# A four-wide second projection group in the first mixer unit, and later HGRN2 threads

## The chip, the cores and the metric

The kernel is one launch on one core of a Trainium2 chip. The metric is device time in microseconds (us) of one execution. The engines are named as in the profile: PE multiplies matrices into PSUM banks and loads its weights through PEld; DVE and ACT do elementwise work and are the only ones here that empty PSUM banks; POOL clears a few tiles; SP issues all DMAs. Each engine takes its instructions strictly in the order in which the program holds them, and an instruction that must wait for another engine holds up everything behind it on its own engine.

## What is computed

One layer of a decoder trunk, for 272 prompt tokens (16 of them meta tokens) and 8 single sample tokens that share all weights: a SwiGLU half-step, a mixer, a second SwiGLU half-step, each followed by a layer norm. Cut to what matters here:

```python
x = layer_norm(ALPHA * x + 0.5 * swiglu(x, f1_g, f1_u, f1_d), ln1_g, ln1_b)
q_r, k_r, v_r, g_r, q_h, f_h, i_h, g_h, a_r, a_h = jnp.split(x @ w_in, 10, axis=-1)   # 2048 wide each
f = lb + (1 - lb) * sigmoid(f_h);  k_h = 1 - f;  q_h = silu(q_h)
o_r, s_ret = retention(rotary(q_r), rotary(k_r) / 16, v_r, s_ret)                     # 8 heads of 256
o_h, s_hg = hgrn2(q_h, k_h, i_h, log(f), s_hg)                                        # 16 heads of 128
y = sigmoid(a_r) * head_ln(o_r) * silu(g_r) + sigmoid(a_h) * head_rms(o_h) * silu(g_h)
x = layer_norm(ALPHA * x + y @ w_out, ln2_g, ln2_b)
x = layer_norm(ALPHA * x + 0.5 * swiglu(x, f2_g, f2_u, f2_d), ln3_g, ln3_b)
```

The outputs are the new tokens and, for prompt and samples, the final states of both recurrences.

## The kernel before

**Dense work.** Activations stand with features on the 128 partitions and the 280 tokens along the row, in 16 pieces `xh[c]`, `xl[c]`: the high part in fp32r and the rest. Weights come as blocks of 128 x 128, eight to a DMA of 512 KB (`raw`). ACT casts each such unit to `whi` (L145), DVE subtracts to get `wlo` (L147), three buffers of each. `dense` (L162 to L174) multiplies: for each of 16 pieces k, and each block of a group, three matmuls into one PSUM bank, `whi` x `xh`, `whi` x `xl`, `wlo` x `xh` (L169, L170, L171). A group of n blocks is thus 16 steps of 3n matmuls. A matmul streams 280 columns, or 264 where the 16 meta tokens are not needed (the names in `LIVE`).

**PSUM.** Eight banks stand in two pools of four: `acc_bank` for dense outputs, `mx_bank` for the mixer's small matmuls and, of unit 0, for the `i_h` group. A pool hands its banks round; a matmul that starts in a bank waits until the last reader of what it held is through.

**The mixer.** It runs over eight units u, each one retention head and two HGRN2 heads. `project` computes the six projections f, q_h, i_h, q_r, k_r, v_r in groups of two blocks (`qkv_groups`), and, one unit later, the four gates (`gate_groups`). `evacuate` empties the banks. After `i_h` it starts a generator `mix_hg`, after `v_r` one called `mix_ret`: threads that hold the recurrences' small work. `dense` calls `pump` after each step k; `pump` counts each thread down by one and runs it to its next `yield` when its count is out. A `yield 14` therefore means "go on 14 dense steps later". This sets the order on PE, which is the order in which the code runs. DVE, ACT and SP get their order from a scheduler that reads the same code; it is fixed in the built program.

`mix_hg` transposes v (`pt`), after a yield multiplies products against ones (`pd`, and `pl` of its first level), goes through seven levels of a scan (`pl`), and then for each of two heads: transposes K (`ptk`), loads and updates the sample states (`smh`), yields, makes the prompt state (`pst`, copied to `Sh`), yields 10, multiplies queries by the sample states (`pq`), yields 3, makes the output (`po`), yields 7, sums squares (`pv`) and normalises. The gates' `evacuate` needs the threads' outputs: `while u not in done: pump()` (L513) runs a thread on at once, with no dense step between, where it has not finished.

**The start of the mixer.** The first four blocks of unit 0, f and q_h, are multiplied while the first layer norm is unfinished, on data before the mean is taken off; `Norm.first` (L294 to L314) then calls `normalise`, which makes the final `xh[c]` and `xl[c]` for 16 pieces (on DVE L191, L320, L324 for each, on ACT L323), and only then corrects the four outputs: DVE reads each bank in L309 (`pj_f`, `pj_q_h`). These four outputs fill all four banks of `acc_bank`.

Of the kernel before, what the change touches and what calls it, by code (L numbers as in the profile page):

```python
# [20 lines left out]
KC = D // P  # L21
DFF = 5504
FC = DFF // P
NMETA, SEQ, NS = 16, 256, 8
LP = NMETA + SEQ
T = LP + NS
# [39 lines left out]
QKV_ORDER = ["f", "q_h", "i_h", "q_r", "k_r", "v_r"]  # L66
LIVE = {"q_r", "q_h", "g_r", "g_h", "a_r", "a_h"}
# [3 lines left out]
def qkv_groups(u):  # L71
    gs = [[(n, 2 * u), (n, 2 * u + 1)] for n in QKV_ORDER]
    if u == 0:
        gs = [gs[0] + gs[1]] + gs[2:]
    return gs


# [20 lines left out]
def trunk(ctx: ExitStack, tc: tile.TileContext, A, O):  # L98
# [62 lines left out]

    def dense(block, nk, outs, xhi, xlo, cols=slice(0, T), hook=None):  # L162
        n = len(outs)
        for k in range(nk):
            for i in range(n):
                wh, wl = block()
                h, l = xhi[k][:, cols], xlo[k][:, cols]
                o = outs[i][:, : h.shape[1]]
                nc.tensor.matmul(o, wh, h, start=k == 0, stop=False)  # L169
                nc.tensor.matmul(o, wh, l, start=False, stop=False)  # L170
                nc.tensor.matmul(o, wl, h, start=False, stop=k == nk - 1)  # L171
            if hook is not None:
                hook(k)
# [32 lines left out]
    xh = [None] * KC  # L206
    xl = [None] * KC
# [176 lines left out]
    norm1 = ffn(1, A["w_up1"], A["w_dn1"], 1)  # L384


    with tc.tile_pool(name="yp", bufs=1) as yp:
        yh, yl = [None] * KC, [None] * KC
        with tc.tile_pool(name="mp", bufs=1) as mp:
# [27 lines left out]
            block = stream(A["w_in"])  # L417
            st = {}
# [31 lines left out]
            def start(gen, wait):  # L450
                threads.append([gen, wait])

            def project(groups):
                for grp in groups:
                    n = grp[0][0]
                    if len(grp) == 4:
                        outs = norm1.first(block, [acc_bank(f"pj_{n}{c}") for n, c in grp])
                    else:
                        bank = mx_bank if grp[0] == ("i_h", 0) else acc_bank
                        outs = [bank(f"pj_{n}{c}") for n, c in grp]  # L460
                        dense(block, KC, outs, xh, xl, slice(NMETA, T) if n in LIVE else slice(0, T), pump)
                    for j in range(0, len(grp), 2):
                        n = grp[j][0]
                        w0 = NMETA if n in LIVE and len(grp) == 4 else 0
                        w1 = w0 + (TL if n in LIVE else T)
                        evacuate(n, grp[j][1], grp[j + 1][1], outs[j][:, w0:w1], outs[j + 1][:, w0:w1])

            def evacuate(n, c0, c1, o0, o1):
                if n == "f":
                    f = tmp("f", (P, 2, T))  # L470
                    k = tmp("k", (P, 2, T))
# [7 lines left out]
                elif n == "q_h":  # L479
                    q = tmp("q", (P, 2, TL))  # L480
# [4 lines left out]
                elif n == "i_h":  # L485
                    v = tmp("v", (P, 2, T))
                    nc.scalar.copy(v[:, 0, :], o0)
                    nc.scalar.copy(v[:, 1, :], o1)
                    start(mix_hg(c0 // 2, st["f"], st["k"], st["q"], v), 3)
                elif n in ("q_r", "k_r"):  # L490
                    sc, w, x0 = (1.0, TL, NMETA) if n == "q_r" else (KSC, T, 0)
                    r = tmp(n, (P, 2, w))
# [6 lines left out]
                elif n == "v_r":  # L499
                    v = tmp("v", (P, 2, T))  # L500
# [3 lines left out]
                elif n in ("g_r", "g_h"):  # L504
# [7 lines left out]
                    u, e = divmod(c0, 2)  # L512
# [24 lines left out]
            def mix_hg(u, f, k, q, v):  # L537
# [23 lines left out]
                for h in range(2):  # L561
# [5 lines left out]
                    nc.scalar.copy(vm[:NMETA, h], pt[:NMETA, 2 * P :].rearrange("p (b f) -> p b f", b=2))  # L567
                    vrow.append(rows_out(vm[8:16, h, 1, :], P, f"vh{h}"))
                    yield 1
                yield 9 if u else 5  # L570
                pd = mx_bank("pd")
                sums(pd.rearrange("p (i c) -> p i c", i=2), hilo, slice(0, 2))
                nc.vector.tensor_tensor(
# [3 lines left out]
                for s in LEVELS:  # L577
# [5 lines left out]
                    for h in range(2 if s > 2 else 0):  # L583
                        for b in range(2):
                            k0, q0, o = NMETA + b * P, b * P, (2 * h + b) * min(s, 64)
                            if s == 64:
                                nc.tensor.matmul(
                                    pl[0:s, o : o + s], K[:, h, k0 : k0 + s], Q[:, h, q0 + s : q0 + 2 * s],
                                    start=True, stop=True)
# [5 lines left out]
                            else:  # L595
# [4 lines left out]
                                    start=True, stop=True)  # L600
# [4 lines left out]
                    n = LP - k0  # L605
                    nb = n // s
                    m = nb // 2
# [32 lines left out]
                for h in range(2):  # L640
# [14 lines left out]
                            out=sm[:, b, :], in0=vb[:, b, :], scalar=fk[:, 1, h, b : b + 1], in1=sm[:, b, :],  # L655
                            op0=ALU.mult, op1=ALU.add)
                    nc.sync.dma_start(O["sgs"][2 * u + h], sm)
                    yield 14 if u else 6

                    S = tmp("Sh", (P, 3, P))  # L660
                    pst = mx_bank("pst")
# [11 lines left out]
                    for b in range(NS):  # L673
# [3 lines left out]
                            start=b < 4, stop=b >= 4, tile_position=(0, j))  # L677
# [277 lines left out]
```

## Time and profile before

| | |
|---|---|
| median of 3 runs | 2826.17 us (2825.42 to 2827.91) |
| the profiled execution | 2827.42 us, its span in the profile 2825.5 us |
| PE busy | 2789.3 us, 99% of the span, 22642 matmul records |
| DVE, ACT busy | 1725.2 us (61%), 1354.2 us (48%) |
| mean granted PE clock | 0.996 |
| the mixer | about 812 to 1958 us of the span |

The profiled execution's time is 1.9 us more than its span, and 1.25 us more than the median of the runs. A busy time is the union of an engine's records. A matmul's record is longer (0.29 us) than the distance to the next one's start (0.129 us for 280 columns), because matmuls overlap; so time lost on PE is read from the starts. The waits list gives for each kind of instruction the idle time ahead of it and what ended it. The stage view gives busy times, counts and the granted clock of any stretch.

### The profile page before, as it was taken

Reading aid. Unit: us, or ns where it says so; the run is one execution under the profiler, and the core shown is the slowest. Engines: PE = TensorE matmul, PEld = TensorE weight load, DVE = VectorE, ACT = ScalarE, POOL = GpSimd, SP = SyncE. Lnnn points to the kernel's source line nnn. Section 1 sums busy time; section 2 is a strip of 40 time slices with the busy share of each in tenths; the row PEclk is TensorE's granted clock in tenths of the full one; section 3 lists DMA queues with packets and bytes.
Section 4 is the critical chain, followed back from the end, with each engine's and each line's share of the span. In section 5 each row is a group of like instructions: output and inputs, shape, how many; then the busy total and the mean of one; then the engine's idle time right before and its main releaser. Section 6 shows DMA issues by size and latency. Waiting matters only on the chain.

```text
span 2825.5 us, 54397 instructions
## 1 busy us (share of the span) xinstructions
PE 2789.3 (99%) x22642; PEld 2758.0 (98%) x22642; DVE 1725.2 (61%) x2786; ACT 1354.2 (48%) x2035; POOL 4.3 (0%) x42
## 2 busy tenths in 40 slices
PE   8999999999999999999999999999999999999997
PEld 8999999999999999999999999999999999999997
DVE  5444444455578777777777777775984444445555
ACT  4433344333355565656565656564554444443333
POOL 0000000000000000000000000000000000000000
PEclk9999999999999999999999999999999999999998
DMA  6555555555555675757575757575555555555543
GB/s 213 169 171 171 171 172 171 170 167 171 172 172 179 224 249 178 249 178 249 177 250 175 252 175 252 175 249 172 178 180 181 181 183 182 180 184 179 181 181 128
DMA packets 155718, 536.26 MB, mean 190 GB/s; under 512 B 18064, under 2 KB 27856, under 8 KB 155472
## 3 DMA queue, kind: packets, MB, share of 16 engines
q1 hardware_dynamic: 155472, 532.80, 55.5%
q8 instruction: 177, 2.90, 0.4%
q14 instruction: 69, 0.57, 0.1%
HBM read 502.12 MB, written 30.61 MB: 189 GB/s over the span
## 4 chain that ended last, share of the span: by engine, by line
PE 97%; DVE 1%; DMA 1%; ACT 0%; issue 0%; SPq 0%; ACTq 0%; DVEq 0%
PE up L170 12%; PE up L171 12%; PE up L169 12%; PE dn L169 6%; PE dn L170 6%; PE dn L171 6%; PE pj_g_r L169 1%; PE pj_v_r L169 1%; PE pj_f L169 1%; PE pj_g_h L169 1%; PE pj_k_r L169 1%; PE pj_f L170 1%; PE pj_k_r L170 1%; PE pj_v_r L170 1%; PE pj_f L171 1%; PE pj_v_r L171 1%
## 5 line engine op out<-in xcount | busy, mean ns | idle before, releaser
L147 DVE TENSOR_TENSOR wlo<-raw,whi 128x1024 fp32r<-128x1024 f32 x868 | 1062.4, 1224 | 892.4 <-ACT whi L145 889.1
L145 ACT CAST whi<-raw 128x1024 fp32r<-128x1024 f32 x868 | 909.0, 1047 | 1163.9 <-PE up L170 484.9
L169 PE MATMUL up<-xh,whi 128*128 128x280 f32 (+1 forms) x2688 | 773.2, 288 | 8.8 <-ACT xh L176 8.8
L170 PE MATMUL up<-xl,whi 128*128 128x280 f32 (+1 forms) x2688 | 774.5, 288 | 1.0 <-DVE xl L177 1.0
L171 PE MATMUL up<-xh,wlo 128*128 128x280 f32 (+1 forms) x2688 | 773.6, 288 | 0.0
L169 PEld LDWEIGHTS up<-xh,whi 128*128 128x128 f32 x2688 | 506.8, 189 | 9.0 <-ACT xh L176 9.0
L170 PEld LDWEIGHTS up<-xl,whi 128*128 128x128 f32 x2688 | 506.4, 188 | 1.8 <-DVE xl L177 1.8
L171 PEld LDWEIGHTS up<-xh,wlo 128*128 128x128 f32 x2688 | 506.7, 189 | 0.0
L169 PE MATMUL dn<-hh,whi 128*128 128x280 f32 (+1 forms) x1376 | 397.1, 289 | 0.0
L170 PE MATMUL dn<-hl,whi 128*128 128x280 f32 (+1 forms) x1376 | 395.8, 288 | 0.0
L171 PE MATMUL dn<-hh,wlo 128*128 128x280 f32 (+1 forms) x1376 | 395.7, 288 | 0.0
L170 PEld LDWEIGHTS dn<-hl,whi 128*128 128x128 f32 x1376 | 259.0, 188 | 0.1
L169 PEld LDWEIGHTS dn<-hh,whi 128*128 128x128 f32 x1376 | 258.9, 188 | 0.1
L171 PEld LDWEIGHTS dn<-hh,wlo 128*128 128x128 f32 x1376 | 258.7, 188 | 0.0
L169 PE MATMUL pj_g_r<-xh,whi 128*128 128x264 f32 x256 | 79.1, 309 | 0.0
L170 PE MATMUL pj_i_h<-xl,whi 128*128 128x280 f32 x256 | 75.5, 295 | 1.6 <-DVE xl L324 1.5
L169 PE MATMUL pj_v_r<-xh,whi 128*128 128x280 f32 x256 | 76.6, 299 | 0.0
L169 PE MATMUL pj_i_h<-xh,whi 128*128 128x280 f32 x256 | 75.5, 295 | 0.3 <-ACT xh L323 0.3
L169 PE MATMUL pj_g_h<-xh,whi 128*128 128x264 f32 x256 | 75.7, 296 | 0.0
L169 PE MATMUL pj_k_r<-xh,whi 128*128 128x280 f32 x256 | 75.2, 294 | 0.0
L171 PE MATMUL pj_i_h<-xh,wlo 128*128 128x280 f32 x256 | 75.2, 294 | 0.0
L171 PE MATMUL pj_v_r<-xh,wlo 128*128 128x280 f32 x256 | 74.6, 292 | 0.0
(328 smaller groups left out, 5195.0 us busy)
## 6 DMA issues: line engine op xcount, KB each, us to landing
raw<-in_w_up SPq DMA_DIRECT2D x344, 512.0 KB, 3.5
raw<-in_w_in SPq DMA_DIRECT2D x320, 512.0 KB, 3.6
raw<-in_w_dn SPq DMA_DIRECT2D x172, 512.0 KB, 3.5
smr<-in_sr SPq DMA_DIRECT2D x32, 512.0 KB, 5.5
out_srs<-smr SPq DMA_DIRECT2D x32, 512.0 KB, 4.3
raw<-in_w_out SPq DMA_DIRECT2D x32, 512.0 KB, 3.5
smh<-in_sg SPq DMA_DIRECT2D x16, 512.0 KB, 3.5
out_sgs<-smh SPq DMA_DIRECT2D x16, 512.0 KB, 4.1
```

Source lines behind the costliest of these rows:

```text
L145: nc.scalar.copy(hi, raw)
L147: nc.vector.tensor_tensor(out=lo, in0=raw, in1=hi.bitcast(F32), op=ALU.subtract)
L169: nc.tensor.matmul(o, wh, h, start=k == 0, stop=False)
L170: nc.tensor.matmul(o, wh, l, start=False, stop=False)
L171: nc.tensor.matmul(o, wl, h, start=False, stop=k == nk - 1)
```

## The change

1. `qkv_groups(0)` joins i_h and q_r into one group of four blocks, as f and q_h are. `dense` takes one range of columns per output, `project` chooses the bank by block: i_h still in `mx_bank`, q_r in `acc_bank`. The layout of `w_in` follows from the same lists. Unit 0 has 16 dense steps fewer.
2. The HGRN2 threads of units 1 to 7 start 40 steps after their i_h is emptied, not 3.
3. Three waits inside `mix_hg` grow: ahead of `pd` 9 to 12 steps (unit 0: 5 to 9), ahead of `pst` in unit 0 6 to 8.

```diff
 def qkv_groups(u):
     gs = [[(n, 2 * u), (n, 2 * u + 1)] for n in QKV_ORDER]
     if u == 0:
-        gs = [gs[0] + gs[1]] + gs[2:]
+        gs = [gs[0] + gs[1], gs[2] + gs[3]] + gs[4:]
     return gs
...
     def dense(block, nk, outs, xhi, xlo, cols=slice(0, T), hook=None):
         n = len(outs)
+        if isinstance(cols, slice):
+            cols = [cols] * n
...
-                h, l = xhi[k][:, cols], xlo[k][:, cols]
+                h, l = xhi[k][:, cols[i]], xlo[k][:, cols[i]]
...
-                    n = grp[0][0]
-                    if len(grp) == 4:
-                        outs = norm1.first(block, [acc_bank(f"pj_{n}{c}") for n, c in grp])
+                    lead = grp[0] == (QKV_ORDER[0], 0)
+                    bank = {("i_h", 0): mx_bank, ("i_h", 1): mx_bank}
+                    outs = [bank.get(m, acc_bank)(f"pj_{m[0]}{m[1]}") for m in grp]
+                    if lead:
+                        outs = norm1.first(block, outs)
                     else:
-                        bank = mx_bank if grp[0] == ("i_h", 0) else acc_bank
-                        outs = [bank(f"pj_{n}{c}") for n, c in grp]
-                        dense(block, KC, outs, xh, xl, slice(NMETA, T) if n in LIVE else slice(0, T), pump)
+                        dense(block, KC, outs, xh, xl, [slice(NMETA if n in LIVE else 0, T) for n, _ in grp], pump)
...
-                    start(mix_hg(c0 // 2, st["f"], st["k"], st["q"], v), 3)
+                    start(mix_hg(c0 // 2, st["f"], st["k"], st["q"], v), 40 if c0 else 3)
...
-                yield 9 if u else 5
+                yield 12 if u else 9
...
-                    yield 14 if u else 6
+                    yield 14 if u else 8
```

The changed file has its lines two or three further down: its L171 to L173 are `dense`, L311 reads the four first banks, L322 and L326 are L320 and L324.

**PE at the start of unit 0's second group.** The rows are the last matmul of the four-block first group and what follows. Before:

```order
L171 MATMUL pj_q_h_8640<-xhg_15_8595,wlo_8872 128x282
L169 MATMUL pj_i_h_9030<-xh_0_8900,whi_9034 128x280
L170 MATMUL pj_i_h_9030<-xl_0_8901,whi_9034 128x280
L171 MATMUL pj_i_h_9030<-xh_0_8900,wlo_9036 128x280
L169 MATMUL pj_i_h_9031<-xh_0_8900,whi_9034 128x280
L170 MATMUL pj_i_h_9031<-xl_0_8901,whi_9034 128x280
L171 MATMUL pj_i_h_9031<-xh_0_8900,wlo_9036 128x280
L169 MATMUL pj_i_h_9030<-xh_1_8906,whi_9034 128x280
L170 MATMUL pj_i_h_9030<-xl_1_8907,whi_9034 128x280
```

and now:

```order
L173 MATMUL pj_q_h_8640<-xhg_15_8595,wlo_8872 128x282
L171 MATMUL pj_i_h_9030<-xh_0_8900,whi_9036 128x280
L172 MATMUL pj_i_h_9030<-xl_0_8901,whi_9036 128x280
L173 MATMUL pj_i_h_9030<-xh_0_8900,wlo_9038 128x280
L171 MATMUL pj_i_h_9031<-xh_0_8900,whi_9036 128x280
L172 MATMUL pj_i_h_9031<-xl_0_8901,whi_9036 128x280
L173 MATMUL pj_i_h_9031<-xh_0_8900,wlo_9038 128x280
L171 MATMUL pj_q_r_9032<-xh_0_8900,whi_9036 128x264
L172 MATMUL pj_q_r_9032<-xl_0_8901,whi_9036 128x264
L173 MATMUL pj_q_r_9032<-xh_0_8900,wlo_9038 128x264
L171 MATMUL pj_q_r_9033<-xh_0_8900,whi_9036 128x264
```

Before, all 96 matmuls of i_h come first and go to `mx_bank`. Now the two q_r blocks follow the first six matmuls of i_h, and their banks are those that held `pj_f`.

**DVE at the same place**, towards the end of `normalise`, up to the read of the first `pj_f` bank (`ls` is the output). Before, from the weight row ahead of `xl_12` on:

```order
L147 TENSOR_TENSOR wlo_9161<-raw_9157,whi_9159 128x8x128
L324 SCALAR_TENSOR_TENSOR xl_12_8973<-d_8055,lnp,xh_12_8972 128x280
L320 SCALAR_TENSOR_TENSOR d_8236<-d_8236,lnp,rr 128x280
L191 TENSOR_TENSOR d_8411<-d_8411,lnc 128x280
L191 TENSOR_TENSOR d_8586<-d_8586,lnc 128x280
L320 SCALAR_TENSOR_TENSOR d_8411<-d_8411,lnp,rr 128x280
L147 TENSOR_TENSOR wlo_9233<-raw_9229,whi_9231 128x8x128
L324 SCALAR_TENSOR_TENSOR xl_13_8979<-d_8236,lnp,xh_13_8978 128x280
L324 SCALAR_TENSOR_TENSOR xl_14_8985<-d_8411,lnp,xh_14_8984 128x280
L320 SCALAR_TENSOR_TENSOR d_8586<-d_8586,lnp,rr 128x280
L309 SCALAR_TENSOR_TENSOR ls_8996<-lnc,wgb,pj_f_8637 128x280
L309 SCALAR_TENSOR_TENSOR ls_9002<-lnc,wgb,pj_f_8638 128x280
```

and now, from the row behind `xl_10` on:

```order
L322 SCALAR_TENSOR_TENSOR d_7880<-d_7880,lnp,rr 128x280
L193 TENSOR_TENSOR d_8055<-d_8055,lnc 128x280
L193 TENSOR_TENSOR d_8236<-d_8236,lnc 128x280
L326 SCALAR_TENSOR_TENSOR xl_11_8967<-d_7880,lnp,xh_11_8966 128x280
L322 SCALAR_TENSOR_TENSOR d_8055<-d_8055,lnp,rr 128x280
L322 SCALAR_TENSOR_TENSOR d_8236<-d_8236,lnp,rr 128x280
L193 TENSOR_TENSOR d_8411<-d_8411,lnc 128x280
L326 SCALAR_TENSOR_TENSOR xl_12_8973<-d_8055,lnp,xh_12_8972 128x280
L326 SCALAR_TENSOR_TENSOR xl_13_8979<-d_8236,lnp,xh_13_8978 128x280
L322 SCALAR_TENSOR_TENSOR d_8411<-d_8411,lnp,rr 128x280
L193 TENSOR_TENSOR d_8586<-d_8586,lnc 128x280
L311 SCALAR_TENSOR_TENSOR ls_8996<-lnc,wgb,pj_f_8637 128x280
```

The three `wlo` rows that stood among these pieces (two are shown, the third stands ahead of `xl_10`) have moved behind them, and the read of `pj_f` stands ahead of `xl_14`. Behind it come `xl_14`, the last L322, L187 on `ls`, and then L311 of the second `pj_f` bank.

**PE at the end of the mixer**, around the last HGRN2 head of unit 7. Before, the `pq` of that head stands among gate matmuls:

```order
L170 MATMUL pj_a_r_22303<-xl_3_8919,whi_22306 128x264
L171 MATMUL pj_a_r_22303<-xh_3_8918,wlo_22308 128x264
L675 MATMUL pq<-smh,qdh 32x128 x8
L169 MATMUL pj_g_r_22302<-xh_4_8924,whi_22347 128x264
L170 MATMUL pj_g_r_22302<-xl_4_8925,whi_22347 128x264
L171 MATMUL pj_g_r_22302<-xh_4_8924,wlo_22349 128x264
L169 MATMUL pj_a_r_22303<-xh_4_8924,whi_22347 128x264
```

and now, behind the last matmul of the gates g_h, a_h of block 14:

```order
L173 MATMUL pj_a_h_22385<-xh_15_8990,wlo_22520 128x264
L665 MATMUL pst<-vm,km 128x128
L666 MATMUL pst<-vth,kth 128x128
L667 MATMUL pst<-vth,kth 128x128
L678 MATMUL pq<-smh,qdh 32x128 x8
L687 MATMUL po<-acch,vth 128x128
L688 MATMUL po<-Q,Sh 128x128
L687 MATMUL po<-acch,vth 128x128
L688 MATMUL po<-Q,Sh 128x128
L689 MATMUL po<-sel,osh 128x8
L184 MATMUL pv<-hhi,ones_r 128x264
L184 MATMUL pv<-hlo,ones_r 128x264
```

The next row now is the first matmul of the gates of block 15 (`pj_g_r`). The thread of unit 7 has 144 dense steps between its i_h and the place where its output is needed (48 of q_r, k_r, v_r, 64 of gates 6, 32 of gates 7). It takes 3 + 2 + 9 + 44 + 2 x 34 = 126 steps before, and 40 + 2 + 12 + 44 + 2 x 34 = 166 now; the last 22 have no dense step between them.

More of the change, by code (lines that the diff above doesn't have):

```diff
@@ L454, in project @@
                 for grp in groups:
-                    n = grp[0][0]
-                    if len(grp) == 4:
-                        outs = norm1.first(block, [acc_bank(f"pj_{n}{c}") for n, c in grp])
-                    else:
-                        bank = mx_bank if grp[0] == ("i_h", 0) else acc_bank
-                        outs = [bank(f"pj_{n}{c}") for n, c in grp]
-                        dense(block, KC, outs, xh, xl, slice(NMETA, T) if n in LIVE else slice(0, T), pump)
+                    lead = grp[0] == (QKV_ORDER[0], 0)
[3 more added lines that the diff above has]
+                        outs = norm1.first(block, outs)
+                    else:
+                        dense(block, KC, outs, xh, xl, [slice(NMETA if n in LIVE else 0, T) for n, _ in grp], pump)
                     for j in range(0, len(grp), 2):
                         n = grp[j][0]
-                        w0 = NMETA if n in LIVE and len(grp) == 4 else 0
+                        w0 = NMETA if n in LIVE and lead else 0
                         w1 = w0 + (TL if n in LIVE else T)
```

## Prediction

> **What bounds the kernel now.** I read the page's busy times first, then the stages of the mixer, then PE's list of waits, then PE's and DVE's rows in order of time at each of them.
>
> ```profile
> span 2825.5 us, 54397 instructions
> PE 2789.3 (99%) x22642; PEld 2758.0 (98%) x22642; DVE 1725.2 (61%) x2786; ACT 1354.2 (48%) x2035; POOL 4.3 (0%) x42
> ...
> L147 DVE TENSOR_TENSOR wlo<-raw,whi 128x1024 fp32r<-128x1024 f32 x868 | 1062.4, 1224 | 892.4 <-ACT whi L145 889.1
> L145 ACT CAST whi<-raw 128x1024 fp32r<-128x1024 f32 x868 | 909.0, 1047 | 1163.9 <-PE up L170 484.9
> ```
>
> PE is the bound, so the change is worth what it takes from or adds to the time in which PE stands still or runs slow. Two stages, in the form of the stage view (stretch, length, PE busy with its count, ..., granted clock, DMA):
>
> ```profile
> 850.00:992.00 142.00, 136.64 (x1097) 131.64 (x1098) 112.59 (x249) 77.97 (x149) 0.00 (x0) 0.98 0.58 199
> 992.00:1133.50 141.50, 141.50 (x1187) 138.19 (x1186) 101.41 (x193) 82.20 (x144) 0.00 (x0) 1.00 0.62 213
> ```
>
> The second row is unit 1 and on: PE is busy throughout, at full clock. In units 1 to 7 there is nothing to win. In the first row 90 matmuls fewer fit into the same time. All that the mixer loses lies there, and the waits list names where:
>
> ```profile
> PE pd L182 <- ACT prodsmh L176: 2.7, 2, 2.0
> ...
> PE pj_i_h L170 <- DVE xl L324: 1.5, 1, 1.5
> PE pst L662 <- ACT km L646: 1.4, 1, 1.4
> PE pd L182 <- DVE prodvbh L177: 1.2, 1, 1.2
> ...
> PE pj_i_h L169 <- ACT xh L323: 0.3, 1, 0.3
> ```
>
> Each costs more than its idle time, since a matmul's record runs past the next one's start. The starts (us, duration, what) give the price:
>
> ```profile
> 837.30 0.30 PE L169 MATMUL pj_i_h<-xh,whi 128*128 128x280 f32 x1
> 846.57 0.29 PE L169 MATMUL pj_i_h<-xh,whi 128*128 128x280 f32 x1
> 853.92 0.30 PE L169 MATMUL pj_q_r<-xh,whi 128*128 128x264 f32 x1
> 862.16 0.28 PE L171 MATMUL pj_q_r<-xh,wlo 128*128 128x264 f32 x1
> 864.99 0.50 PE L182 MATMUL pd<-prodvbh,ones_r 128*128 128x512 f32 x1
> 865.33 0.28 PE L182 MATMUL pl<-prodsmh,ones_r 128*128 128x256 f32 x1
> 937.07 0.29 PE L171 MATMUL pj_i_h<-xh,wlo 128*128 128x280 f32 x1
> 938.71 0.49 PE L662 MATMUL pst<-vm,km 128*128 128x128 f32 x2 [1.36 <-ACT km L646]
> 963.93 0.28 PE L171 MATMUL pj_q_r<-xh,wlo 128*128 128x264 f32 x1
> 967.15 0.41 PE L182 MATMUL pl<-prodsmh,ones_r 128*128 128x256 f32 x1
> ```
>
> From 837.30 to 846.57 stand 72 matmuls of i_h, 0.129 us each. The whole group of 96 should take 12.4 us and took 16.6: **4.2 lost** to `xl`, which `normalise` on DVE does not deliver fast enough. At `pd` of unit 0, 3.17 us passed from 862.16 to 865.33 for one slot of q_r (0.12) and two of 0.34 as between the last two rows there: **2.4 lost**. At `pst`, 1.64 less 0.13: **1.5 lost**. At `pd` of unit 1, 3.22 less 0.80: **2.4 lost**. Then the clock:
>
> ```profile
> 847.10:850.52 3.42, 1.60 (x9) 1.17 (x10) 3.42 (x8) 1.59 (x3) 0.00 (x0) 1.00 0.43 153
> 850.52:853.93 3.41, 3.41 (x17) 3.41 (x17) 3.41 (x10) 0.92 (x2) 0.00 (x0) 0.50 0.46 154
> 860.76:864.17 3.41, 1.69 (x14) 1.47 (x13) 3.14 (x9) 1.59 (x3) 0.00 (x0) 1.00 0.45 155
> 963.16:966.57 3.41, 1.56 (x11) 1.05 (x9) 3.17 (x7) 2.06 (x5) 0.00 (x0) 1.00 0.32 126
> 966.57:969.98 3.41, 3.41 (x14) 3.31 (x15) 3.20 (x9) 0.83 (x2) 0.00 (x0) 0.50 0.53 154
> ```
>
> These stretches lie on one grid of 3.41 us. After one in which PE was busy 1.60 or 1.56 us the next ran at half clock, after one of 1.69 it did not, and a stretch busy throughout ended the slow one. The first slow stretch is inside the 4.2; the second costs half its length, **1.7**. The mixer loses 4.2 + 2.4 + 1.5 + 2.4 + 1.7 = 12.2 us.
>
> **The change part by part.** It neither adds nor removes arithmetic: PE has the same matmuls in another order, SP the same transfers. The 16 `pump` calls that go from unit 0 cost nothing, since no thread lived then.
>
> *The four-wide group* uses a pair of `xh`, `xl` every 12 matmuls (1.5 us) instead of every 6, so the waits for `xl` go: −4.2. But q_r now starts in the banks of `pj_f` after six matmuls, and DVE reads those banks only behind `normalise`, in L309 (now L311). Before, q_r came 96 matmuls later and never met this. When does DVE get there? Its rows before:
>
> ```profile
> 838.27 0.81 DVE L191 TENSOR_TENSOR d<-d,lnc 128x280 f32<-128x280 f32 x2
> 838.99 1.23 DVE L147 TENSOR_TENSOR wlo<-raw,whi 128x1024 fp32r<-128x1024 f32 x1
> 840.13 0.93 DVE L320 SCALAR_TENSOR_TENSOR d<-d,lnp,rr 128x280 f32<-128x280 f32 x2
> 840.97 0.45 DVE L191 TENSOR_TENSOR d<-d,lnc 128x280 f32<-128x280 f32 x1
> 841.33 0.51 DVE L324 SCALAR_TENSOR_TENSOR xl<-d,lnp,xh 128x280 fp32r<-128x280 f32 x1
> ...
> 850.82 0.91 DVE L309 SCALAR_TENSOR_TENSOR ls<-lnc,wgb,pj_f 128x280 f32<-128x280 f32 x2
> ```
>
> Up to `xl_9` (841.33) both orders agree. From start to start an L191 takes 0.36, an L320 or L324 0.42. Now there follow up to the read of `pj_f` four of L324 (`xl_10` to `xl_13`), four of L320 and four of L191: 841.75 + 8 x 0.42 + 4 x 0.36 = 846.55. The read itself takes 0.49 and PE hears of it by 847.1. PE has done its six matmuls at 837.30 + 0.77 = 838.07: **+9.0**. Bounds: 8.5, and 10 if ACT's `xh` comes late behind each pair. The second `pj_f` is read behind `xl_14`, an L320 and a product: 846.97 + 1.20 + 0.49, so 848.7; PE has three matmuls to do meanwhile (0.4): **+1.2**. Behind this wait stands all of PE; weights cannot be late, since their three buffers are full by then, and the next `wlo` moved behind `pj_q_h` has 63 matmuls of cover.
>
> The clock is half when PE comes back at 847.1, as the stretches before were idle. The one to 850.52 then holds about 2.7 us of work, more than 1.69, so I expect full clock from 850.52: 1.8 us at half rate, with matmuls to do from 848.7, **+0.8**; if that stretch doesn't count as busy, 1.7 more. The Trainium skill's "TensorE: Matmul & The Clock Gate", section "What's actually happening", lets the gate fall to half rate after at least one idle window of about 3.4 us and rise after at least one busy one. The trace agrees on length and rate; it differs in that 1.60 us of work did not count as busy here. By that rule read strictly, 847.10 to 850.52 is no busy window and the slow time lasts to 853.93: the sum would be 1.7 us higher.
>
> *The later threads and longer waits.* `pd` of unit 0 now stands 14 steps after the thread's start, in k_r, when DVE made its products long before; `pst` of unit 0 has 8 steps, 5.9 us; `pd` of unit 1 stands in the gates. So −2.4, −1.5, −2.4 and −1.7, all covered by 30 and more matmuls. If that cover fell short, 1.5 to 2.4 each would stay. New is a close call at the first `pvr` (retention of unit 0): between the copies of `por` and the cast `rhi` ACT has two weight casts (1.05 each), a table load (1.28, quoted below) and eight short rows of about 0.35, and DVE a row of 0.43, some 6.6 us, against 48 slots or 6 us of PE: **+0.5**, from 0 to the 1.5 of the `pst` row.
>
> *The end of the mixer.* The thread of unit 7 is now driven without dense work through `pst`, `pq`, `po`, `pv`:
>
> ```profile
> 1905.22 1.28 ACT L199 ACT_TABLE_LOAD   x1
> ...
> 1915.26 0.39 ACT L688 ACTIVATE sqh<-po 128x264 f32<-128x264 f32 x1 [0.46 <-PE po L686]
> ...
> 1904.08 0.72 DVE L667 SCALAR_TENSOR_TENSOR Sh<-Sh,T,pst 128x128 f32<-128x128 f32 x2
> 1916.27 0.43 DVE L177 TENSOR_TENSOR hlo<-sqh,hhi 128x264 fp32r<-128x264 f32 x1 [1.00 <-ACT hhi L176]
> ...
> 1911.19 0.65 PE L675 MATMUL pq<-smh,qdh 128*32 128x128 f32 x16
> 1914.05 0.38 PE L684 MATMUL po<-acch,vth 128*128 128x128 f32 x2
> 1914.94 0.29 PE L686 MATMUL po<-sel,osh 128*128 128x8 f32 x2
> ```
>
> Count from the last gate matmul. On DVE `Sh`, which `po` needs, now stands behind a `wlo` and a gate product; that `wlo` needs a `whi` whose buffer comes free only at that moment. So 0.1 + 1.05 (`whi`) + 1.2 (`wlo`) + 0.35 + 0.4 (`Sh`) = 3.1, then the rest of `po` (0.5), then from `sqh` to the end of `hlo` 1916.70 − 1915.26 = 1.44, then `pv`: PE is back at the gates after 5.3. Its own work in it is `pst` (three pairs of 0.22, as in `po`), `pq` 0.6, `po` 1.1, `pv` 0.24, together 2.6: **+2.7**. Bounds: 1.8 if `Sh` isn't held up, 4 if another weight unit gets between; a half-clock stretch would add 1.7, if one grid stretch holds less than some 1.6 us of this work.
>
> Sum: 9.0 + 1.2 + 0.8 + 0.5 + 2.7 − 12.2 = **+2.0 us** on the profiled execution's 2827.42, which is 1.25 above the median of 2826.17; so I forecast a median of 2828.2. The change trades waits for waits.
>
> **The rivals.** *Slower, by units 1 to 7.* HGRN2's `pd` and first levels now fall among retention's transposes, and the second `pt` of k_r waits for DVE after 1.2 us of PE work behind `pd` (two slots of `pl`, three transposes, six gate matmuls).
>
> ```profile
> 865.54 0.68 DVE L573 TENSOR_TENSOR acch<-pd,ident 128x512 f32<-128x512 f32 x1
> ```
>
> DVE needs 0.68 of these 1.2 to read `pd`. If the `wlo` ahead of it (1.22) runs 0.5 late, PE waits in every unit, up to 1 us, and 7 x 1 gives 2835. Against: DVE is busy 101 of 141.5 us in a unit. For: its work now falls closer together.
>
> *Faster, because the bank wait is short.* If DVE got to `pj_f` within 3 us, the two bank terms and their clock would shrink from 11.0 to about 3 and the time be 2820. The point is DVE's read before about 841; the order puts twelve rows of 0.36 to 0.42 ahead of it, which are fixed.
>
> *The clock stays slow longer*, after the bank wait or at the end: 1.7 for either, 2830 to 2831.6.
>
> *The change doesn't do what it says*: one or two of the waits at `pd`, `pst` stay, as a transfer late on ACT's queue can hold `km`: 2831 to 2833.
>
> **How the numbers follow.** Within 0.2% (5.65 us) is about what a measurement of this kernel cannot tell from no change. The forecast has 0.55, with its own range 2825.5 to 2831; the longer slow clock 0.13; waits that stay 0.08; units 1 to 7 0.19; the short bank wait 0.05. The last alone is faster by more than 0.2%. Slower by more are the units 1 to 7, and the clock and the waits that stay where the terms' upper bounds add to them, 0.11 between them. So faster 0.05, same 0.65, slower 0.30. The range reaches from 2825, the lower bounds of the terms, to 2837, where seven waits and some clock meet.
>
> **What would show it.** The waits list of the changed kernel should have q_r at its first matmul waiting about 9 us for DVE's `ls`, then again about 1 us; no `pj_i_h`, `pd` or `pst` wait of unit 0; `po` and `pv` near 1930 us; a half-clock stretch up to 850.5 and none near 966. Units 1 to 7 should take 141.4 us each with PE busy throughout; a repeated wait of one kind, seven times, would make me wrong on the slow side, a q_r wait under 4 us on the fast side.

## The result and the profile after

The changed kernel takes 2835.61 us (median of 8 runs, 2833.76 to 2837.72), the kernel before, run with it on the same chip, 2827.69 us. The ratio is 1.0028, with a 95% interval from 1.0017 to 1.0038: the change makes the kernel slower by about 8 us. The profiled execution took 2833.76 us, 6.3 more than the one of before.

The head of the page, then two stages in the form of the stage view (stretch, length, PE busy with its count, PEld, DVE, ACT and POOL likewise, granted clock, DMA share and rate):

```profile
span 2832.0 us, 54408 instructions
PE 2789.4 (98%) x22642; PEld 2757.6 (97%) x22642; DVE 1718.1 (61%) x2786; ACT 1351.4 (48%) x2033; POOL 4.3 (0%) x42
```

```profile
850.00:992.00 142.00, 140.75 (x1153) 137.09 (x1152) 106.98 (x221) 73.49 (x137) 0.00 (x0) 0.99 0.62 202
992.00:1133.50 141.50, 141.36 (x1184) 137.82 (x1183) 100.19 (x193) 80.85 (x142) 0.00 (x0) 1.00 0.67 213
```

PE's busy time is the same to 0.1 us and the span 6.5 longer. The stretch from 850 us, which before had only 136.64 us of PE work in it, is now nearly full: the waits of before are gone. The next stretch is no longer quite full. The waits list of PE in the changed kernel (waiter, what it waited for, us in total, times, longest) shows the new ones; the rows left out are waits of the first SwiGLU and norm, alike in both kernels:

```profile
PE pj_q_r L171 <- DVE ls L311: 9.6, 2, 9.0
...
PE pvr L184 <- DVE rlo L179: 1.2, 1, 1.2
PE pv L184 <- ACT hhi L178: 1.1, 1, 1.1
...
PE po L688 <- DVE Sh L670: 0.7, 1, 0.7
```

None of `pj_i_h`, `pd` and `pst` is left. The largest new one, row by row on PE (start, duration, what, and in brackets the idle time and what ended it), and the row of DVE that it waits for:

```profile
837.47 0.29 PE L173 MATMUL pj_i_h<-xh,wlo 128*128 128x280 f32 x1
846.74 0.56 PE L171 MATMUL pj_q_r<-xh,whi 128*128 128x264 f32 x1 [8.98 <-DVE ls L311]
...
848.36 0.56 PE L171 MATMUL pj_q_r<-xh,whi 128*128 128x264 f32 x1 [0.62 <-DVE ls L311]
```

```profile
846.09 0.50 DVE L311 SCALAR_TENSOR_TENSOR ls<-lnc,wgb,pj_f 128x280 f32<-128x280 f32 x1
...
847.71 0.50 DVE L311 SCALAR_TENSOR_TENSOR ls<-lnc,wgb,pj_f 128x280 f32<-128x280 f32 x1
```

Six matmuls after i_h begins PE stops for 9.1 us, until DVE has read the first `pj_f` bank, and then for 0.9 more. The clock in those stretches:

```profile
842.80:846.21 3.41, 0.00 (x0) 0.00 (x0) 3.41 (x10) 1.31 (x3) 0.00 (x0) 0.50 0.00 1
846.21:849.62 3.41, 2.27 (x9) 2.02 (x9) 3.41 (x10) 2.29 (x4) 0.00 (x0) 0.50 0.00 0
849.62:853.04 3.42, 3.42 (x17) 3.42 (x16) 2.72 (x10) 1.67 (x4) 0.00 (x0) 0.50 0.00 0
853.04:856.45 3.41, 3.41 (x29) 3.41 (x29) 3.20 (x6) 1.52 (x3) 0.00 (x0) 1.00 0.31 78
```

PE is back at 846.74 and runs at half rate until 853.04. Summed over the starts of its matmuls, that costs 2.5 us.

The waits list leaves out the seven short waits of units 1 to 7. They stand in the view of the tile `pd`, whose bank is read by DVE and waited for by the transposes of k_r; below it unit 1, in order of time:

```profile
who waited for it (us, times):
  PEld pt L732: 2.5, 7
```

```profile
999.82 1.22 DVE L147 TENSOR_TENSOR wlo<-raw,whi 128x1024 fp32r<-128x1024 f32 x1 [0.53 <-ACT whi L145]
...
1000.54 0.40 PE L184 MATMUL pd<-prodvbh,ones_r 128*128 128x512 f32 x1
...
1001.65 0.68 DVE L576 TENSOR_TENSOR acch<-pd,ident 128x512 f32<-128x512 f32 x1
...
1002.39 0.55 PE L732 MATMUL pt<-ident,k_r 128*128 128x128 f32 x3
```

DVE reads `pd` at 1001.65, behind a weight product that itself waited 0.53 for ACT, and behind two short rows of retention (`vs` and `ks`) that take the 0.6 us in between. By the starts PE loses 0.29 to 0.31 in each of the seven units, 2.1 together.

All losses in one table, from the distances of PE's matmul starts, for the stretch from the first matmul of the mixer's first group to the first of `w_out`:

| us | before | after |
|---|---|---|
| i_h waits for `xl`, with the half clock inside | 4.2 | 0 |
| `pd` and `pst` of unit 0, `pd` of unit 1 | 2.4 + 1.5 + 2.4 | 0 |
| half clock near 966 | 1.7 | 0 |
| q_r waits for the banks of `pj_f` | 0 | 9.1 + 0.9 |
| half clock behind it | 0 | 2.5 |
| first `pvr` | 0 | 1.5 |
| `pt` of k_r, seven times | 0 | 2.1 |
| `po`, `pv` of unit 7 | 0 | 0.9 + 1.2 + 0.35 |
| sum | 12.2 | 18.5 |
| length of the stretch | 1145.7 | 1152.6 |

The sum grows by 6.3 and the stretch by 7.0; the other 0.7 lies in gaps under 0.25 us.

### The profile page after: what moved, and what is told of

Read it like the earlier page. It is cut to its first block, busy times and chain, and to the rows that moved or that the text cites. A ratio compares the mean times of both kernels' runs of the same rounds, so it can differ in the third digit from the quotient of the medians.

```text
span 2832.0 us, 54408 instructions
## 1 busy us (share of the span) xinstructions
PE 2789.4 (98%) x22642; PEld 2757.6 (97%) x22642; DVE 1718.1 (61%) x2786; ACT 1351.4 (48%) x2033; POOL 4.3 (0%) x42
## 4 chain that ended last, share of the span: by engine, by line
PE 97%; DVE 2%; ACT 1%; DMA 0%; issue 0%; SPq 0%; ACTq 0%; DVEq 0%
PE up L172 12%; PE up L173 12%; PE up L171 12%; PE dn L171 6%; PE dn L172 6%; PE dn L173 6%; PE pj_i_h L171 1%; PE pj_f L171 1%; PE pj_g_h L171 1%; PE pj_g_r L171 1%; PE pj_k_r L171 1%; PE pj_i_h L172 1%; PE pj_f L172 1%; PE pj_v_r L172 1%; PE pj_k_r L172 1%; PE pj_f L173 1%
## 5 line engine op out<-in xcount | busy, mean ns | idle before, releaser
L171 PE MATMUL up<-xh,whi 128*128 128x280 f32 (+1 forms) x2688 | 773.0, 288 | 8.7 <-ACT xh L178 8.7
L173 PE MATMUL up<-xh,wlo 128*128 128x280 f32 (+1 forms) x2688 | 773.5, 288 | 0.0
L171 PEld LDWEIGHTS up<-xh,whi 128*128 128x128 f32 x2688 | 506.6, 188 | 8.9 <-ACT xh L178 8.9
L173 PEld LDWEIGHTS up<-xh,wlo 128*128 128x128 f32 x2688 | 506.5, 188 | 0.0
L171 PE MATMUL dn<-hh,whi 128*128 128x280 f32 (+1 forms) x1376 | 397.1, 289 | 0.0
L173 PE MATMUL dn<-hh,wlo 128*128 128x280 f32 (+1 forms) x1376 | 395.7, 288 | 0.0
L171 PEld LDWEIGHTS dn<-hh,whi 128*128 128x128 f32 x1376 | 258.9, 188 | 0.1
L173 PEld LDWEIGHTS dn<-hh,wlo 128*128 128x128 f32 x1376 | 258.7, 188 | 0.0
L171 PE MATMUL pj_q_r<-xh,whi 128*128 128x264 f32 x256 | 73.7, 288 | 9.6 <-DVE ls L311 9.6
L171 PE MATMUL pj_g_r<-xh,whi 128*128 128x264 f32 x256 | 78.7, 308 | 0.0
L171 PE MATMUL pj_i_h<-xh,whi 128*128 128x280 f32 x256 | 77.1, 301 | 0.0
L171 PE MATMUL pj_g_h<-xh,whi 128*128 128x264 f32 x256 | 75.8, 296 | 0.0
L171 PE MATMUL pj_v_r<-xh,whi 128*128 128x280 f32 x256 | 75.6, 295 | 0.0
L173 PE MATMUL pj_i_h<-xh,wlo 128*128 128x280 f32 x256 | 75.0, 293 | 0.0
L171 PE MATMUL pj_k_r<-xh,whi 128*128 128x280 f32 x256 | 74.8, 292 | 0.0
```

## The experiments

Theory: the four-wide group pays with the bank wait and the slow clock behind it, and the later threads pay with `pvr`, `pt` and the end of the mixer. What was open is which part removed the old waits. Each run stood on one chip with the kernel before, whose median was 2827.1 to 2827.3 us on the three chips used; the ratios are to that. A span is about 2 us less than its time, and where an expectation is of the span, the span is given too.

### Where q_r goes, and when the banks are read

**q_r in the mixer's banks** (against the changed kernel):

```diff
-                    bank = {("i_h", 0): mx_bank, ("i_h", 1): mx_bank}
+                    bank = {(n, c): mx_bank for n in ("i_h", "q_r") for c in (0, 1)}
```

> The changed kernel, with the two q_r blocks of unit 0's four-wide group in the pool that also takes i_h, so that they do not wait for the banks of the first group. Theory (bank wait): the waits of 9.1 and 0.9 us for DVE's two reads and the half-clock time behind them (2.5 us lost) go together, 12.5 us; span 2832.0 - 12.5 = 2819.5, 0.2% under the kernel before; no half clock near 840 to 853. Rival (DVE's pace): DVE cannot make the normalised pieces fast enough for any group that starts there, so PE waits for xl instead; at least the 4.2 us of the kernel before come back and the span is 2824 or more.

Measured: 2822.2 us against 2827.2, ratio 0.9984 [0.9975, 0.9994]; the profiled span is 2820.2, 0.7 over what was expected. PE has neither a q_r wait nor an `xl` wait, and the clock is full throughout the mixer.

**The banks read ahead of most of the work of `normalise`:**

```diff
-            self.normalise()
             ys = []
             for i, o in enumerate(outs):
+                if i == (2 if self.which == 1 else 0):
+                    self.normalise()
```

> The changed kernel, with DVE's reads of the first two banks written ahead of the normalisation of the 16 pieces, the banks as in the changed kernel. Theory (bank wait, set by the place of the read in DVE's order): PE waits for q_r's banks by less than 2 us or not at all, the clock stays up, and the span is 2819.5 to 2821, as with the other banks. Rival (DVE's pace): the six moved instructions (2.4 us) make all 16 pieces late, PE waits for xl by 2 us and more, 2824 or above.

Measured: 2823.0 us, ratio 0.9982 [0.9973, 0.9992]; the profiled span is 2820.1, as expected. The mixer's rows of the waits list of this kernel, and DVE's reads in it (both `pj_f` banks in one row of the merged view):

```profile
PE pvr L184 <- DVE rlo L179: 1.2, 1, 1.2
PE pv L184 <- ACT hhi L178: 1.1, 1, 1.1
PE po L689 <- DVE Sh L671: 0.7, 1, 0.7
```

```profile
837.25 0.94 DVE L312 SCALAR_TENSOR_TENSOR ls<-lnc,wgb,pj_f 128x280 f32<-128x280 f32 x2
```

The two edits touch different things, the bank and the order on DVE, and both take the q_r wait and every slow stretch behind it away. So the wait is for the bank, its length is the place of the read in DVE's queue, and the slow clock follows from the wait: 10.1 + 2.5 = 12.6 us. With q_r in the mixer's banks the mixer's stretch is 12.4 us shorter (1140.2 for 1152.6); the medians, from different sets of runs, differ by 13.4. No `xl` wait comes in its place, so DVE keeps up with a four-wide group.

### The two parts of the change, each alone

**The later threads and longer waits alone** (the groups of unit 0 as before):

```diff
-        gs = [gs[0] + gs[1], gs[2] + gs[3]] + gs[4:]
+        gs = [gs[0] + gs[1]] + gs[2:]
```

> The kernel before with the later thread starts and the longer thread waits alone; the second group stays two wide. Theory: the waits for xl stay (4.2 us), pd of unit 0 shrinks from 2.4 to under 1, the waits at pst, at pd of unit 1 and the half clock behind it go (1.5, 2.4, 1.7); the waits of the later threads come: 0.3 us in each of units 1 to 7 (2.1), 2.4 at the end, up to 1.5 at the first pvr. Span 2825.5 - 7.2 + 5 = 2823.5, between 2822.5 and 2825. Rival (the threads are what makes the changed kernel slow): 2829 or more.

Measured: 2828.5 us, ratio 1.0004 [0.9995, 1.0014]. The profiled span is 2827.3; expected was a span of 2823.5. The mixer's rows of the waits list but one, then the stage view near the end of the mixer:

```profile
PE pj_i_h L170 <- DVE xl L324: 1.5, 1, 1.5
PE pv L182 <- ACT hhi L176: 1.1, 1, 1.1
PE pd L182 <- DVE prodvbh L177: 1.0, 1, 1.0
PE po L685 <- DVE Sh L667: 0.7, 1, 0.7
PE pv L182 <- DVE hlo L177: 0.4, 1, 0.4
```

```profile
1930.55:1933.97 3.42, 1.58 (x10) 1.09 (x9) 2.72 (x8) 1.28 (x4) 0.20 (x2) 1.00 0.56 183
1933.97:1937.38 3.41, 3.41 (x18) 3.41 (x18) 0.95 (x4) 2.19 (x3) 0.10 (x1) 0.50 0.03 8
```

The waits for `xl` stay, as they should. The longer waits do take away `pst`, `pd` of unit 1 and the half clock there, but of `pd` of unit 0 1.2 us remain. Against that stand seven `pt` waits (2.0), the end (2.4), a half-clock stretch behind it (1.7) and a new 0.6 at a `pv`. Of the 3.8 us that the span is over the expected one, the clock at the end (1.7), that `pv` (0.6) and 0.4 of `pd` beyond what I had left for it were not in the expectation, and the 0.5 that it held for `pvr` did not come: 2.2 together. The other 1.6 I did not trace.

**The four-wide group alone**, with unit 1's thread set back by the 16 steps that unit 0 loses, so that the threads of units 0 and 1 stay as far apart as before:

```diff
-                    start(mix_hg(c0 // 2, st["f"], st["k"], st["q"], v), 40 if c0 else 3)
+                    start(mix_hg(c0 // 2, st["f"], st["k"], st["q"], v), 19 if c0 == 2 else 3)
...
-                yield 12 if u else 9
+                yield 9 if u else 5
...
-                    yield 14 if u else 8
+                    yield 14 if u else 6
```

> The changed kernel with the four-wide group alone: the threads' waits are those of before, and unit 1's thread starts 19 steps after its i_h is emptied, 3 plus the 16 dense steps that unit 0 no longer has. Theory (the group costs the time, by the bank wait): the bank waits of q_r as in the changed kernel (9.1 and 0.9), about 2.5 us at half clock behind them, no wait of i_h for xl (-4.2) and, since PE comes to pd of unit 0 about 10 us later than DVE has its products, no wait there (-2.4); pst of unit 0, pd of unit 1 and the half clock at 966 stay: 2827.2 + 9.1 + 0.9 + 2.5 - 4.2 - 2.4 = 2833.1. No seven waits at pt of k_r and none at the end. Rival (the later threads and longer waits cost it): close to the kernel before, 2827 or less.

Measured: 2827.2 us against 2827.3, ratio 1.0001 [0.9992, 1.0010]. The expectation failed, by 6 us. The waits list of the whole kernel:

```profile
PE pj_q_r L171 <- DVE ls L311: 9.6, 2, 9.0
PE up L171 <- ACT xh L178: 8.9, 2, 8.6
PE p L287 <- DVE ls L190: 1.9, 1, 1.9
PE up L172 <- DVE xl L179: 1.0, 2, 0.7
```

The bank wait is there as expected, and of the mixer's old waits not one is left: `pst`, `pd` of unit 1 and the half clock, 5.6 us that I had let stand, are gone, though no thread is later but that of unit 1, by its 16 steps. This kernel pays 12.6 and saves 12.2. So the changed kernel's 8 us over this one come from the threads: `pvr` 1.5, `pt` 2.1 and the end 2.4 are 6.0, and the rest, 0.9 of 6.9 in the traces of the mixer, lies in gaps under 0.25 us.

**The group alone, with q_r in the mixer's banks.** Did the old waits go because PE stood still for 10 us while DVE went on, or because of the group's order?

```diff
-                    bank = {("i_h", 0): mx_bank, ("i_h", 1): mx_bank}
+                    bank = {(n, c): mx_bank for n in ("i_h", "q_r") for c in (0, 1)}
```

> The four-wide group alone, as in the earlier run (2827.2, bank waits of q_r 9.1 and 0.9, slow clock behind them, no other wait in the mixer), with q_r of unit 0 in the mixer's banks. Theory (the bank wait itself removed the waits of unit 0, since DVE went on for 10 us while PE stood): the bank wait goes (-10.1 and -2.5 of clock), and pd (2.4) and pst (1.5) of unit 0 come back, perhaps pd of unit 1 with its half clock (4.1): 2818.5 to 2822.7. Rival (the group's 16 dense steps fewer and their other order on DVE and ACT removed them, whatever PE waits for): 2827.2 - 12.6 = 2814.6 with no wait left.

Measured: 2815.3 us against 2827.1, ratio 0.9958 [0.9944, 0.9972]. The rival of the expectation holds: it is the order, not PE's standing still. The waits list is that of the group alone without its first row: PE has no wait left in the mixer, and the clock is full throughout it.

How `pd` of unit 0 lost its wait is seen on PE and DVE in this kernel, and on DVE in the kernel before:

```profile
861.72 0.29 PE L171 MATMUL pj_k_r<-xh,whi 128*128 128x280 f32 x1
...
870.33 0.40 PE L184 MATMUL pd<-prodsmh,ones_r 128*128 128x512 f32 x1
870.57 0.39 PE L184 MATMUL pd<-prodvbh,ones_r 128*128 128x512 f32 x1
```

```profile
859.00 0.37 DVE L313 TENSOR_SCALAR rt<-rt,wgb 128x280 f32<-128x280 f32 x1
...
869.32 0.78 DVE L179 TENSOR_TENSOR prodvbh<-pr,prodsmh 128x256 fp32r<-128x256 f32 x2
```

```profile
857.20 0.36 DVE L311 TENSOR_SCALAR rt<-rt,wgb 128x280 f32<-128x280 f32 x1
...
864.18 1.09 DVE L177 TENSOR_TENSOR prodvbh<-pr,prodsmh 128x256 fp32r<-128x256 f32 x3
```

The thread starts when its group is through, at 861.72 here and at 853.92 before. The L313 row (L311 before) is the last of the four first outputs; until then DVE has `normalise` and these outputs to do. Here that ends at 859.4, ahead of the thread's start; before it ended at 857.6, 3.6 us behind it. So the products are done at 870.1, 8.4 us after the start, and `pd` comes 8.6 us after it; before they were done at 865.3, 11.4 us after the start, and PE stood at `pd` from 8.4 us on. The group moved the thread by 7.8 us and DVE's backlog by 1.8 only, and so did what the longer `yield` ahead of `pd` was to do.

`pst` went for two reasons, on ACT and on PE:

```profile
932.24 0.49 PE L644 MATMUL ptk<-ident,K 128*128 128x128 f32 x3
...
937.46 1.05 ACT L780 ACTIVATE smr<-smr 128x1024 f32<-128x1024 f32 x1
938.42 0.24 ACT L646 COPY km<-ptk 16x128 f32<-16x128 f32 x1
```

```profile
939.21 0.49 PE L647 MATMUL ptk<-ident,K 128*128 128x128 f32 x3
...
942.40 0.24 ACT L649 COPY km<-ptk 16x128 f32<-16x128 f32 x1
```

(The first block is of the kernel before, the second of this one.) In both a table load stands ahead of `km`. Before, a weight cast and two rows of retention's sample states (`smr`, the second is shown) stand there too, 3.1 us, and `km` begins 6.2 us after the transposes; here it begins 3.2 us after them. On PE, two groups of retention's `por` matmuls, about 1 us each, now stand between the transposes and `pst`, which begins 6.9 us after them; before, PE was ready for it after 5.0. Both go back to one thing: between the start of unit 0's HGRN2 thread and that of its retention there are 16 dense steps fewer, so retention is further along. Its second `pqr` begins 11.2 us behind these transposes before, and 5.2 us ahead of them here.

`pd` of unit 1 is not settled so. Before, it stood 3.3 us behind retention's first `pvr`; here it stands 17.7 us behind it. But the group hardly changes how far unit 1's i_h is from unit 0's retention (that `pvr` begins 29.1 us after the first matmul of i_h before, 27.0 here); it is unit 1's thread that starts 16 steps later after its i_h. The run of the threads alone lost this wait and its half clock too, 4.1 us, with a later thread and without the group. So the later start is the likelier cause, but no run has the wide group with unit 1's thread at 3 steps.

The four runs fit one sum. This kernel's stretch from the first matmul of the mixer to `w_out` is 1133.1 us with no wait in it. With 12.2 us of old waits it would be 1145.3 (before: 1145.7), with 12.6 of bank and clock 1145.7 (group alone: 1145.7), and with 12.6 and 6.0 1151.7 (changed kernel: 1152.6).

### The threads' own waits

**All later threads at 18 steps instead of 40:**

```diff
-                    start(mix_hg(c0 // 2, st["f"], st["k"], st["q"], v), 40 if c0 else 3)
+                    start(mix_hg(c0 // 2, st["f"], st["k"], st["q"], v), 18 if c0 else 3)
```

> The changed kernel with the HGRN2 threads of units 1 to 7 starting 18 steps after i_h, not 40. Theory: the thread of unit 7 is through when it is needed, so the waits at the end (2.4 us) go, and pd no longer falls among retention's transposes, so the seven waits of 0.3 us go; the bank wait stays. Span 2832.0 - 4.5 = 2827.5. Rival: unit 1's thread now starts while that of unit 0 still runs and shares its buffers, and a new wait of 1 to 3 us at po or pq of unit 0 takes back part of it: 2829 to 2831, but nothing repeated in units 2 to 7.

With 18 steps, unit 1's thread begins while unit 0's still runs and writes its sample queries into `qdh` (at 947.18 us) before unit 0's second head has read its own (its `pq` starts at 975.51), so part of the sample tokens' result is computed from mixed data; the amount of work is the same. Measured: 2843.0 us, ratio 1.0053 [1.0038, 1.0068], 7 us above the changed kernel where I had expected less than that one. The `pt` waits of units 1 to 7 and the waits at the end are gone, as they should be. In their place:

```profile
PE po L689 <- ACT osh L682: 2.7, 1, 2.7
...
PE pqr L795 <- DVE smr L786: 1.7, 3, 0.9
```

The first, at 979 us where the two threads meet, was followed by a half-clock stretch (1.7). The list shows of `pqr` only its three longest waits. By the starts of its 16 matmuls, the second `pqr` of units 1 to 7 takes 1.8 to 3.3 us where it takes 1.0 in the changed kernel, 8.4 us in all: the matmuls wait one after the other for their piece of `smr` (in the view of that tile their weight loads wait 16 times, 6.7 us; in the changed kernel never), and most of it lies in gaps under 0.25 us. With `po` (2.8) and 1.9 more of half clock, less the 4.5 that went, that makes 8.6; the mixer's stretch grew by 8.0. Why `smr` comes late there was not traced.

**`pd` two steps later still**, with q_r in the mixer's banks (compare 2822.2 above):

```diff
-                yield 12 if u else 9
+                yield 14 if u else 9
```

> The changed kernel with q_r of unit 0 in the mixer's banks (as in the earlier run, 2822.2) and pd of units 1 to 7 two steps later, 14 for 12, so that it stands behind both transposes of k_r and not between the two. Theory (the second transpose waits 0.3 us in each of seven units for the bank that DVE still reads in acch<-pd): the seven waits go, 2822.2 - 2.1 = 2820.1, and the threads end two steps later, which the end of the mixer may pay with up to 0.3. Rival (the 0.3 us belong to the transposes themselves, as retention's small matmuls wait there in any order): 2822.2, with seven waits at another pt or at pl.

Measured: 2824.1 us against 2827.3, ratio 0.9988 [0.9979, 0.9997], some 2 us more than without the two steps and not 2 less. The view of the tile `acch`, which DVE writes in reading `pd`:

```profile
L576 DVE TENSOR_TENSOR acch<-pd,ident x8: 681/682/684, 874.2 to 1843.0; 128x512 f32<-128x512 f32 x8
...
who waited for it (us, times):
  PEld psc L749: 3.5, 7
```

The second transpose of k_r waits no more; `psc`, which stands next in the mixer's banks, does, 0.44 to 0.47 in each unit. The cause is the read of `pd` late on DVE, and whatever comes next in that pool pays. The mixer's end keeps its 2.4 and is now followed by a half-clock stretch, 1.7.

**Only the last thread at 18 steps**, again with q_r in the mixer's banks:

```diff
-                    start(mix_hg(c0 // 2, st["f"], st["k"], st["q"], v), 40 if c0 else 3)
+                    start(mix_hg(c0 // 2, st["f"], st["k"], st["q"], v), (40 if c0 < 14 else 18) if c0 else 3)
```

> The changed kernel with q_r of unit 0 in the mixer's banks, and of the HGRN2 threads the last alone, that of unit 7, starts 18 steps after its i_h is emptied and not 40. Theory (the end of the mixer pays 2.4 us because the thread is driven without dense work): no wait of po and pv near 1930 us, 2822.2 - 2.4 = 2819.8, and as pd of unit 7 falls ahead of the transposes, 0.3 less at pt: 2819.5. Rival (an earlier thread only moves the waits, as the run with 18 steps in all units had some 0.4 us more in every later unit): 2821.5 to 2822.2, with waits of po or pqr in unit 7.

Measured: 2821.0 us, ratio 0.9978 [0.9969, 0.9987]. `po`, `pv` and the `pt` of unit 7 are gone, 2.7 us; in their place the second `pqr` of unit 7 takes 2.6 us where it took 1.0. Of the 2.7, 1.2 arrived.

**Both together, q_r in the mixer's banks, and the first `pvr` three steps later:**

```diff
-                    start(mix_hg(c0 // 2, st["f"], st["k"], st["q"], v), 40 if c0 else 3)
+                    start(mix_hg(c0 // 2, st["f"], st["k"], st["q"], v), (40 if c0 < 14 else 18) if c0 else 3)
...
-                yield 12 if u else 9
+                yield 14 if u else 9
...
-                yield 7
+                yield 7 if u else 10
```

> All together: q_r of unit 0 in the mixer's banks, pd of units 1 to 7 at 14 steps, the last thread at 18, and ahead of the first pvr 10 steps for 7. Theory (each of the waits left is separate): 2822.2 - 2.1 - 2.4 - 1.5 = 2816.2 (of the 2.4 and the 2.1 the wait of pt in unit 7 counts in one only), with no PE wait over 0.25 us in the mixer: that is 11 us less than the kernel before. Rival (waits trade places, as in the change itself): 2819 or more, with a new wait of po, pv or pqr.

Measured: 2819.0 us, ratio 0.9969 [0.9958, 0.9981]. `pvr` and the end are free; the second `pqr` of unit 7 takes 1.8 us for 1.0, and six `psc` waits of 0.45 stay:

```profile
PE psc L749 <- DVE acch L576: 1.7, 6, 0.3
```

**The longer waits in unit 0 alone**, q_r in the mixer's banks, units 2 to 7 as before:

```diff
-                    start(mix_hg(c0 // 2, st["f"], st["k"], st["q"], v), 40 if c0 else 3)
+                    start(mix_hg(c0 // 2, st["f"], st["k"], st["q"], v), 30 if c0 == 2 else 3)
...
-                yield 12 if u else 9
+                yield 9
...
-                yield 7
+                yield 7 if u else 10
```

> The four-wide group with q_r in the mixer's banks, and the longer waits in unit 0 alone: pd at 9 and pst at 8 steps as in the changed kernel, the first pvr at 10 for 7, unit 1's thread at 30 so that it doesn't meet that of unit 0; units 2 to 7 start at 3 and have pd at 9 as before. Theory (in units 2 to 7 the later threads remove nothing and cost 0.5 us a unit, 141.9 against 141.4, and the end 2.4): 2818.9, the best so far, less 6 x 0.5 = 2816, units 2 to 7 at 141.4 and no wait at the end. Rival (a wait comes back in unit 1 or 2, whose threads are now closer together): 2818 to 2821, with pd or po named in unit 1.

Measured: 2816.7 us against 2827.1, ratio 0.9963 [0.9950, 0.9975]. Units 2 to 7 are back at 141.4 us each, and no wait at the end; in unit 1 one `pl` waits 0.8 and the second `pqr` takes 0.7 longer. It is not below the 2815.3 of the group with no longer wait at all. So with the four-wide group none of the longer waits is needed, beyond the 16 steps of unit 1's thread. The group with q_r in the mixer's banks and no more than these 16 steps is the fastest kernel of the study, 12 us under the kernel before.

## Why the prediction was right or wrong

The time lies in the range, 2825 to 2837; but my likeliest case, no measurable change at 2828.2, was wrong. The kernel is slower, by 0.28%, a case to which I gave 0.30.

- **Bank wait, +9.0 and +1.2:** right, 9.1 and 0.9. Counting DVE's rows to 846.55 was off only by the 0.47 that this execution started earlier (846.09 by its row).
- **"So I expect full clock from 850.52 ... +0.8":** mis-sized, it measured 2.5. The step that failed is that a stretch with 2.7 us of work would end the slow time because 1.69 had been enough not to begin one. The stretch in which PE came back, at another phase than in the kernel before, held 2.27 and did not; only the next one, busy throughout, did. The sentence on the Trainium skill's "TensorE: Matmul & The Clock Gate", section "What's actually happening", read strictly (a busy window is needed to rise), gave 1.7 more: that is what the trace shows.
- **First `pvr`, +0.5:** 1.5, its upper bound. ACT, which I had counted, was in time: `rhi` is ready at 961.36, when PE is. On DVE a weight product goes ahead of `rlo`, and for DVE I had counted only the 0.43 of `rlo` itself:

```profile
961.44 1.22 DVE L147 TENSOR_TENSOR wlo<-raw,whi 128x1024 fp32r<-128x1024 f32 x1
962.57 0.43 DVE L179 TENSOR_TENSOR rlo<-sqr,rhi 128x264 fp32r<-128x264 f32 x1
```

- **Units 1 to 7, 0:** wrong; 0.3 each, 2.1. The rival named the mechanism, the second `pt` of k_r behind DVE's read of `pd`, and its point, a weight product 0.5 late: it was 0.53 late. The two rows of retention behind that product, 0.6 us, I had not counted. The rival's price of up to 1 us a unit was too high. A margin of half a microsecond behind a queue with rows of 1.2 us should not have been taken as a cover.
- **End of the mixer, +2.7:** 2.4, by the rows named.
- **Removed waits, −12.2:** right in size, and all went. But I put 8.0 of it down to the later threads and longer waits. The wide group with the old waits and unit 1's thread 16 steps later is without all 12.2: the 8.1 of unit 0 go with the group, the 4.1 of unit 1 with it or with that later start. What the threads' part does beyond this removes nothing and costs 6.9. The step behind it is "the 16 `pump` calls that go from unit 0 cost nothing, since no thread lived then": before, the 16 steps of q_r ran beside unit 0's HGRN2 thread, and without them retention is further along, which took `pst` away. That the total of 12.2 came out is luck in part: I had counted each wait once, and two parts of the change aim at the same ones.

By terms: 2.0 + 1.7 (clock) + 1.0 (`pvr`) + 2.1 (`pt`) − 0.3 (end) − 0.1 (bank) = 6.4; the mixer grew by 7.0, the difference being the small gaps, and the two profiled executions differ by 6.3. The range held because the three larger misses were rivals or bounds that I had priced; their chance was too low because I treated small margins as covered one by one, and all of them went the same way.

## What to carry to other kernels

When a change widens a group, look at what its new outputs overwrite and how far down another engine's queue the last read of that stands; here a different bank was worth 12 to 13 us and cost nothing. When a change has two parts that aim at the same waits, run each alone: the wider group had already moved unit 0's thread away from the backlog, and of the second part only a shorter delay of unit 1's thread may have been of use; the rest only cost time. A wait that was taken out at one instruction in a ring of banks went to the next user of the ring (0.3 us at `pt` became 0.45 at `psc`), as the late read itself came no earlier.

## What the hardware showed that was not expected

- The granted clock falls and rises at different points. It fell after stretches of 3.41 us with 1.56 to 1.65 us of PE work (five of them), and in the run with 18 steps after one with 1.70; it stayed full after 1.69, 1.79 and 1.91. So near 1.7 us the busy time doesn't decide it to the last hundredth. Once at half, stretches with 2.14 and 2.27 us did not bring it back, nor did one with 2.80 in the run with 18 steps, in the stage view:

```profile
847.42:850.84 3.42, 2.80 (x12) 2.52 (x12) 3.42 (x10) 2.68 (x4) 0.00 (x0) 0.50 0.00 0
850.84:854.25 3.41, 3.41 (x17) 3.41 (x16) 2.71 (x7) 1.69 (x3) 0.00 (x0) 0.50 0.00 0
```

- The stretches lie at another phase in each execution, so the same wait of 9.1 us gave 10.2 us of half clock in the changed kernel and 13.7 in the run with 18 steps, and the same waits at the end of the mixer gave a half-clock stretch in two kernels (threads alone, `pd` at 14) and none in others.
